# Even layer's seams: statistics later, one more gate block beside the Fourier stage, attention units at a smaller distance, the last heads read last

## The chip, the core and the metric

The kernel runs on one core of one Trainium2 chip. A core has TensorE (PE, the matmuls), VectorE (DVE), ScalarE (ACT), GpSimd (POOL) and SyncE (SP), which issues the DMAs. Each engine works through its own queue in order, and semaphores hold an instruction until what it reads is there. The metric is the device time of one execution, in microseconds (us).

## What is computed

A two-layer encoder over 768 positions (a sequence of 256 and one of 512) and 2048 channels. The change touches layer 0, the even one: one input projection feeds 12 query heads in 4 groups (each with one key and one value head), attention in a window of 128 positions, and 4 groups of Fourier mixing; each branch is multiplied by the SiLU of a gate projection, and one output projection adds to the residual. Cut from the reference:

```python
def _even_layer(x, g, w_in, w_out, q_gain, k_gain, sink, w_f, b_f, rel_bias):
    z = _rmsnorm(x, g) @ w_in
    q, k, v, f, ga, gf = _split(z, EVEN_SPLITS)
    q = _rmsnorm(q.reshape(B, S, N_HEADS, HEAD_DIM), q_gain)
    k = _rmsnorm(k.reshape(B, S, N_KV_HEADS, HEAD_DIM), k_gain)
    a = _window_attention(q, k, v, rel_bias, sink) * jax.nn.silu(ga)
    fo = _fourier(f, w_f, b_f) * jax.nn.silu(gf)
    return x + jnp.concatenate([a, fo], axis=-1) @ w_out
```

## The kernel before

Channels lie on the 128 partitions, positions run along the free axis (T = 768, two halves of H = 384). Every fp32 operand is split into a high and a low part (`split`: a copy on ACT, line 133, and a subtraction on DVE, line 134), and each product is three matmuls (`three`, by `mm`, line 119). The input tiles lie in numbered slots; weights arrive in raw tiles `wr` and are split into `wh` and `wl`, four ahead of their use.

The order on PE is written out by the program: the order of the calls is the order of the queue. Side work is written as generators that a small planner (`Pipe`) holds in a heap. Its clock `pipe.now` counts PE work only: 0.425 ns a column (at least 252 columns) for a matmul, 0.107 a transpose. After each step of the main stream, `tick` runs the generators that are due, and `yield 3.5` means "go on 3.5 units later". `flush` runs what is left, with no main work in between. ACT, DVE and SP are ordered by the scheduler from these calls.

What follows one another in layer 0 around the change:

- The QK pairs and a pair of gates, in a Strassen form (`strassen`). For each of 16 blocks and each half, `Normed.squares` (line 625 on) squares on ACT, adds on DVE, and puts the high and low parts into one tile `st2`; 3.5 units later the matmul with `pick` adds it into one row of `stat`.
- The Fourier stage, pool `fnet`: the roots of the statistics become `rstk` (high part in rows 0 to 15, low part in rows 32 to 47, of 48). `chan_mix` multiplies w_f with the channel transform (L714), `tables` loads and splits the position tables and the Fourier input (`th`, `tl`, `fh`, `fl`), and `fourier` multiplies them. All loads of this stage share four buffers named `row`. Beside it run gate blocks 0 and 1 (`ga_block`, 96 matmuls of 384 columns, of kind `slot,wh` and `slot,wl`, each).
- Attention, pool `attn`: 4 head groups of 6 units. A unit (`attend`) makes its q from `rstk` and a selector `sel` (three matmuls of 48 rows and 128 columns), then scores (`kh,qh`), softmax on DVE and ACT, transposes (`ident,sc`, L129) and products with v (`pth,vh`). Unit i starts at `at - 8 + UNITS_AT * i`. A group's keys take two `rstk,sel` matmuls of 384 columns. After a group's last unit `gates` loads the SiLU gates and multiplies them in (`gate`, L353); for the last group the product is kept on the chip. Gate blocks 2 to 11 are the main stream.
- The first out projection (`Out`): `load_cat` loads and splits the 16 concatenated blocks (two halves each) into slots; the four plain output blocks are done as two duos (`duo`), each by quarters of four blocks; `build_sums` (L394 to L397, and splits) makes the sums for the Strassen pairs after them on DVE.

Of the kernel before, what the change touches and what calls it, by code (L numbers as in the profile page):

```python
# [10 lines left out]
F32 = mybir.dt.float32  # L11
F32R = mybir.dt.float32r
# [5 lines left out]
P = 128  # L18
# [22 lines left out]
QLATE = (2, 3, 0, 1)  # L41
FIRST_UNIT, UNITS_AT = 14.0, 10.2
PT_AT, PV_AT = 7.89, 13.07
# [51 lines left out]
def trunk(ctx, tc, x_t, w_in_e, w_fn, w_vn, w_out_e, w_in_o, w_sv, w_out_o, w_f, w_st, b_s, sink, rel_bias,  # L95
# [62 lines left out]
    nc.scalar.activation(out=pick[:, 15:16], in_=ident[:, 0:1], func=AF.Copy, scale=0.0, bias=1.0)  # L158
    twin = const.tile([48, 16], F32, name="twin")
    nc.vector.tensor_add(out=twin, in0=ident[0:48, 0:16], in1=ident[0:48, 32:48])  # L160
    qg = const.tile([P, 1], F32, name="qg")
# [66 lines left out]
    def out_order(src, layer, pairs):  # L228
        plain = [(src, layer, b, q) for i in range(0, len(PLAIN), 2) for q in range(4) for b in PLAIN[i:i + 2]]
        return plain + [(src, layer, b, q) for b in pairs for q in range(14)]  # L230
# [79 lines left out]
    class Stream:  # L310
# [20 lines left out]

        def duo(self, bs, tags, done):

            for q in range(4):
                weights.ahead(weights.at[self.n, bs[0], q] + RING)
                for k in range(4 * q, 4 * q + 4):
                    for s in range(2):
                        for b, t in zip(bs, (tags[:2], tags[2:])):
                            self.step(b, k, s, t[s], k == 0, k == KT - 1)
                        if done:  # L340
                            done(k, s)
# [30 lines left out]

    def ev():
        return late[-1].tile([P, H], F32, name="ev", bufs=4)

    def extra(dtype=F32):

        return slot(spare[0], dtype) if lent[0] else ev()

# [39 lines left out]
    class Out:  # L419

        def __init__(self, n, pairs, first, last, res, result):
            self.n, self.pairs, self.res, self.result = n, pairs, res, result
            self.tags = (first, last, first)

        def run(self):
# [10 lines left out]
            for i, tags in zip(range(0, len(PLAIN), 2), self.tags):  # L438
                duo = PLAIN[i:i + 2]
                last = i + 2 == len(PLAIN)  # L440
                if last:
                    pipe.flush()
                st.duo(duo, tags, done if last else None)
                for b in duo:
                    for h, z in enumerate(st.take(b)):
                        res = ev()
                        nc.sync.dma_start(out=res, in_=self.res[b][:, SL[h]])
                        nc.vector.tensor_add(out=res, in0=z, in1=res)
                        self.result(b, h, res)
# [140 lines left out]
    with tc.tile_pool(name="early", bufs=1, reuse_waits="tile") as pool:  # L590
# [10 lines left out]
        duo = (GF0, GF0 + 1)  # L601
        st.duo(duo, (6, 7, 0, 1), None)
        for g, b in enumerate(duo):
# [15 lines left out]
        class Normed:  # L619
# [7 lines left out]
            def squares(self, i, h, t):  # L627
# [4 lines left out]
                nc.vector.tensor_add(out=a, in0=a, in1=b)  # L632
                st2 = extra(F32R)
                nc.scalar.copy(out=st2[0:64], in_=a)
                nc.vector.tensor_sub(out=st2[64:P], in0=a, in1=st2[0:64].bitcast(F32))  # L635
                yield 3.5
                mm(stat[h], pick[:, 15 - i:31 - i], st2, i + h == 0 if h == 0 else i == 1, i == 15 - h, True)
# [44 lines left out]
    mid = shared.__enter__()  # L682
    rstk = mid.tile([48, T], F32R, name="rstk")
    banks["z"], banks["s"] = itertools.cycle((0, 1, 4)), itertools.cycle((6, 2, 7, 3, 5))
# [8 lines left out]
    with tc.tile_pool(name="fnet", bufs=1, reuse_waits="tile") as pool:  # L693
        rows.append(pool)
        inv = pool.tile([16, T], F32, name="inv")
        nc.scalar.activation(out=rstk, in_=rr[0:48], func=AF.Copy, scale=0.0)
        for s in range(2):
# [97 lines left out]
        pipe.spawn(tables(), 1.0)  # L795
        pipe.spawn(chan_mix(), 8.0)
        for g in range(NF):
            pipe.spawn(ungated(g), 14.0 + 11.0 * g)
        for j in range(2):
            ga_block(j)  # L800
# [3 lines left out]
    with tc.tile_pool(name="attn", bufs=1, reuse_waits="tile") as pool:  # L804
# [6 lines left out]
        class Group:  # L811
# [5 lines left out]
            def load(self):  # L817
# [6 lines left out]
                for j in range(3):  # L824
# [4 lines left out]
                    self.bias.append(t)  # L829
                self.sel = pool.tile([48, 4, P], F32R, name="sel", bufs=2)  # L830
                e = twin[:, 4 * g:4 * g + 4].rearrange("p (n o) -> p n o", o=1)
                nc.scalar.copy(out=self.sel, in_=e.to_broadcast([48, 4, P]))
                yield 6.0
# [20 lines left out]
        def attend(gr, s, qb):  # L854
# [58 lines left out]
            nc.scalar.copy(out=gr.at[:, :, t * P:(t + 1) * P], in_=ps.rearrange("p (j q) -> p j q", j=3))  # L913
            if (s, qb) == (1, SEQS[1][1] - 1):
                yield 1.0
                gr.gates()

        units = [(s, qb) for s in range(2) for qb in range(SEQS[s][1])]
        for g in range(NKV):
# [3 lines left out]
            for i, (s, qb) in enumerate(units):  # L923
                pipe.spawn(attend(gr, s, qb), at - 8.0 + UNITS_AT * i)
        for j in range(2, NQ):
            ga_block(j)
        pipe.flush()
        load_cat([(k, s) for k in range(KT) for s in range(2)])
    shared.__exit__(None, None, None)
# [12 lines left out]
    sums = {i: [None] * KH for i in (1, 2, 3)}  # L942
    Out(1, PAIRS_E, (2, 3, 6, 7), (0, 1, 4, 5), x_t, keep_sum).run()

# [155 lines left out]
    sums = {i: [None] * KH for i in (1, 2, 3)}  # L1100
    Out(3, PAIRS_O, (0, 1, 4, 5), (2, 3, 6, 7), x1, finish).run()

# [80 lines left out]
```

## Time and profile before

| | |
|---|---|
| median of 3 runs | 2181.46 us (2180.48 to 2181.55) |
| the profiled execution | 2179.42 us, its span 2177.6 us |
| PE busy | 2121.1 us, 97% |
| DVE busy | 1486.3 us, 68% |
| ACT busy | 977.2 us, 45% |
| mean granted clock | 0.988 of full speed |

Times in the profile are us from the span's start. A matmul's end is modelled, so its issue interval is the difference of two starts. The granted clock of TensorE is 1.00 at full speed (2.4 GHz) and 0.50 at half (1.2 GHz); a mean between them says how much of a stretch ran at either. Idle time of an engine counts only if the chain that ends last goes through it.

### The profile page before, as it was taken

To read this page: it belongs to the slowest core of one execution; us is meant where nothing else is said; L and a number is where in the kernel's file an instruction comes from. 1 tells how busy PE (TensorE), PEld (TensorE's weight loads), DVE (VectorE), ACT (ScalarE), POOL (GpSimd) and SP (SyncE) were. 2 spreads that over 40 slices of the span, in tenths; PEclk is the share of its full clock that TensorE was granted. 3 is DMA by queue.
4 is the path that set the end of the run, shared out by engine and by line. 5 is a ranking of instruction groups with operands and counts; after the bars stand their busy time and mean duration, and the time that the engine had idled before them with its cause. 6 is when DMAs were issued, how large, how long until landed. Compare 5 with 4: busy or idle time off the path is not lost.

```text
span 2177.6 us, 32105 instructions
## 1 busy us (share of the span) xinstructions
PE 2121.1 (97%) x11778; PEld 2038.8 (94%) x11778; DVE 1486.3 (68%) x2628; ACT 977.2 (45%) x1907; POOL 75.0 (3%) x75
## 2 busy tenths in 40 slices
PE   8999999989999979999899999999999999999999
PEld 6989999988999979999888999999999999999999
DVE  8686666654566678666695666666666778796665
ACT  6345444543566564333624433333334545553332
POOL 5000000000000000112100000000000000000000
PEclk9999999999999989999999999999999999999999
DMA  6884322354333357433856322222222322394342
GB/s 225 250 296 150 103 90 84 97 165 149 107 127 129 101 199 234 157 117 124 279 187 225 114 85 85 78 77 77 70 85 88 112 92 94 120 318 153 124 136 73
DMA packets 158342, 303.55 MB, mean 139 GB/s; under 512 B 16316, under 2 KB 107624, under 8 KB 158184
## 3 DMA queue, kind: packets, MB, share of 16 engines
q1 hardware_dynamic: 158184, 301.51, 42.9%
q8 instruction: 92, 1.51, 0.3%
q14 instruction: 66, 0.54, 0.1%
HBM read 240.08 MB, written 64.51 MB: 140 GB/s over the span
## 4 chain that ended last, share of the span: by engine, by line
PE 83%; DVE 8%; DMA 3%; ACT 3%; issue 2%; SPq 0%; POOL 0%; ACTq 0%; DVEq 0%
PE bank L119 82%; DVE wl L134 2%; DVE slot L277 1%; PE bank L129 1%; DMA slot<-cat 1%; ACT wh L133 1%; DVE slot L134 1%; DVE slot L635 1%; DVE wr L205 0%; DVE wr L207 0%; ACT sc L888 0%; DMA slot<-x 0%; DMA s<-slot 0%; DMA x<-ev 0%; ACT slot L133 0%
## 5 line engine op out<-in xcount | busy, mean ns | idle before, releaser
L119 PE MATMUL bank<-slot,wh 128*128 128x384 f32 x6448 | 1651.0, 337 | 0.8 <-DVE ev L506 0.8
L119 PEld LDWEIGHTS bank<-slot,wh 128*128 128x128 f32 x6448 | 1164.2, 188 | 4.2 <-issue 2.0
L119 PE MATMUL bank<-slot,wl 128*128 128x384 f32 x3224 | 1084.2, 336 | 3.6 <-DVE wl L134 3.5
L133 ACT CAST wh<-wr 128x512 fp32r<-128x512 f32 x782 | 480.4, 619 | 810.5 <-PE bank L119 628.5
L134 DVE TENSOR_TENSOR wl<-wr,wh 128x512 fp32r<-128x512 f32 x782 | 541.4, 696 | 349.4 <-ACT wh L133 329.8
L119 PEld LDWEIGHTS bank<-slot,wl 128*128 128x128 f32 x3224 | 606.5, 188 | 4.6 <-DVE wl L134 4.6
L119 PE MATMUL bank<-wh,slot 128*128 128x512 f32 x768 | 243.9, 397 | 12.5 <-DVE slot L277 7.3
L119 PEld LDWEIGHTS bank<-wh,slot 128*128 128x128 f32 x768 | 145.9, 190 | 46.0 <-DVE slot L277 9.0
L133 ACT CAST slot<-slot 128x384 fp32r<-128x384 f32 x232 | 114.1, 512 | 141.7 <-DVE slot L134 39.2
L119 PE MATMUL bank<-wl,slot 128*128 128x512 f32 x384 | 152.2, 396 | 1.9 <-DVE wl L134 1.9
L134 DVE TENSOR_TENSOR slot<-slot,slot 128x384 fp32r<-128x384 f32 x232 | 127.8, 556 | 37.8 <-ACT slot L133 32.0
L119 PEld LDWEIGHTS bank<-wl,slot 128*128 128x128 f32 x384 | 73.3, 191 | 18.9 <-DVE wl L134 3.1
L207 DVE TENSOR_TENSOR wr<-wr 128x1024 f32<-128x1024 f32 x45 | 58.4, 1299 | 1.2
L209 DVE TENSOR_TENSOR wr<-wr 128x1024 f32<-128x1024 f32 x45 | 55.1, 1225 | 1.5
L203 DVE TENSOR_TENSOR wr<-wr 128x1024 f32<-128x1024 f32 x45 | 55.0, 1221 | 0.8
L205 DVE TENSOR_TENSOR wr<-wr 128x1024 f32<-128x1024 f32 x45 | 54.9, 1221 | 0.7
L500 DVE TENSOR_TENSOR ev<-bank,ev 128x384 f32<-128x384 f32 x45 | 25.1, 557 | 35.0 <-PE bank L119 34.3
L504 DVE TENSOR_TENSOR ev<-bank,ev 128x384 f32<-128x384 f32 x45 | 25.1, 558 | 31.9 <-PE bank L119 31.9
L509 DVE TENSOR_TENSOR ev<-ev,bank 128x384 f32<-128x384 f32 x45 | 24.9, 553 | 30.0 <-PE bank L119 29.7
L938 POOL TENSOR_TENSOR rr<-rr,slot 128x384 f32<-128x384 f32 x24 | 35.3, 1472 | 132.6 <-ACT slot L937 132.6
L888 ACT ACTIVATE sc<-sc,nm 128x256 f32<-128x256 f32 (+1 forms) x72 | 38.3, 533 | 0.4 <-DVE nm L885 0.3
L877 DVE CUSTOM_DVE_ANT_0 sc<-bank,bias 128x256 f32<-128x256 f32 (+1 forms) x72 | 31.0, 466 | 8.5 <-PE bank L119 8.2
(186 smaller groups left out, 1442.3 us busy)
## 6 DMA issues: line engine op xcount, KB each, us to landing
wr<-in_w_in_o_dram SPq DMA_DIRECT2D x96, 512.0 KB, 3.5
wr<-in_w_in_e_dram SPq DMA_DIRECT2D x64, 512.0 KB, 3.7
slot<-cat SPq DMA_DIRECT2D x120, 192.0 KB, 4.1
wr<-in_w_out_e_dram SPq DMA_DIRECT2D x32, 512.0 KB, 3.8
wr<-in_w_out_o_dram SPq DMA_DIRECT2D x32, 512.0 KB, 3.7
slot<-x SPq DMA_DIRECT2D x64, 192.0 KB, 4.4
wr<-in_w_sv_dram SPq DMA_DIRECT2D x16, 512.0 KB, 4.7
slot<-in_x_t_dram SPq DMA_DIRECT2D x32, 192.0 KB, 4.1
```

The source lines that it names most:

```text
L119: nc.tensor.matmul(out, lhsT=lhs, rhs=rhs, start=start, stop=stop, skip_group_check=go_on)
L133: nc.scalar.copy(out=hi, in_=src)
L134: nc.vector.tensor_sub(out=lo, in0=src, in1=hi.bitcast(F32))
L203: nc.vector.tensor_sub(out=w11, in0=w12, in1=w11)
L205: nc.vector.tensor_sub(out=w11, in0=w22, in1=w11)
L207: nc.vector.tensor_sub(out=w12, in0=w22, in1=w12)
L209: nc.vector.tensor_sub(out=w21, in0=w11, in1=w21)
L500: nc.vector.tensor_add(out=u2, in0=p, in1=r1)
L504: nc.vector.tensor_add(out=r1, in0=p, in1=r1)
L877: nc.vector.tensor_tensor_reduce(out=sc[:, j, :nk * P], in0=ps, in1=gr.bias[j][:, bs], scale=1.0, scalar=NEG, op0=ALU.add, op1=ALU.max, ac ...
L888: nc.scalar.activation(out=sc[:, j, :nk * P], in_=sc[:, j, :nk * P], func=AF.Exp, bias=nm[:, j:j + 1], accum_out=den[:, j:j + 1])
L938: nc.gpsimd.tensor_add(out=rr[:, SL[h]], in0=rr[:, SL[h]], in1=sq)
```

## The change

Five things are changed in layer 0. `squares` waits 6.0 units before its matmul instead of 3.5, and takes every second tile for `st2` from the ring `ev` of four. `rstk`, `sel` and `twin` have 128 rows instead of 48 (the rest zeros). `chan_mix` starts at 12 instead of 8, the Fourier groups at 21 + 10g instead of 14 + 11g, and three gate blocks run beside them instead of two. The first unit starts at 13 instead of 14, and the units are 8.3 apart instead of 10.2, beside nine gate blocks instead of ten. The last head group's gates are multiplied after the flush, and the first duo of the first out projection, its weights and the loads of `cat` take the quarters in the order 0, 1, 3, 2, with the last heads (in quarter 2) last.

```diff
-FIRST_UNIT, UNITS_AT = 14.0, 10.2
+LAST_HEADS = (0, 1, 3, 2)
+FIRST_UNIT, UNITS_AT = 13.0, 8.3
...
-    twin = const.tile([48, 16], F32, name="twin")
-    nc.vector.tensor_add(out=twin, in0=ident[0:48, 0:16], in1=ident[0:48, 32:48])
+    twin = const.tile([P, 16], F32, name="twin")
+    nc.vector.tensor_add(out=twin, in0=ident[:, 0:16], in1=ident[:, 32:48])
...
-        plain = [(src, layer, b, q) for i in range(0, len(PLAIN), 2) for q in range(4) for b in PLAIN[i:i + 2]]
+        qs = LAST_HEADS if layer == 1 else range(4)
+        plain = [(src, layer, b, q) for i in range(0, len(PLAIN), 2) for q in (range(4) if i else qs)
+                 for b in PLAIN[i:i + 2]]
...
-        def duo(self, bs, tags, done):
+        def duo(self, bs, tags, done=None, qs=range(4)):
...
-            for q in range(4):
+            for q in qs:
...
-                            self.step(b, k, s, t[s], k == 0, k == KT - 1)
+                            self.step(b, k, s, t[s], k == 4 * qs[0], k == 4 * qs[-1] + 3)
...
-        return slot(spare[0], dtype) if lent[0] else ev()
+        return slot(spare[0], dtype) if lent[0] else ev(dtype)
...
-                st.duo(duo, tags, done if last else None)
+                st.duo(duo, tags, done if last else None, range(4) if i else self.qs)
...
-                st2 = extra(F32R)
+                st2 = extra(F32R) if i % 2 == h else ev(F32R)
...
-                yield 3.5
+                yield 6.0
...
-    rstk = mid.tile([48, T], F32R, name="rstk")
+    rstk = mid.tile([P, T], F32R, name="rstk")
...
-        nc.scalar.activation(out=rstk, in_=rr[0:48], func=AF.Copy, scale=0.0)
+        nc.scalar.activation(out=rstk, in_=rr, func=AF.Copy, scale=0.0)
...
-        pipe.spawn(chan_mix(), 8.0)
+        pipe.spawn(chan_mix(), 12.0)
         for g in range(NF):
-            pipe.spawn(ungated(g), 14.0 + 11.0 * g)
-        for j in range(2):
+            pipe.spawn(ungated(g), 21.0 + 10.0 * g)
+        for j in range(3):
             ga_block(j)
...
-                self.sel = pool.tile([48, 4, P], F32R, name="sel", bufs=2)
+                self.sel = pool.tile([P, 4, P], F32R, name="sel", bufs=2)
...
-                nc.scalar.copy(out=self.sel, in_=e.to_broadcast([48, 4, P]))
+                nc.scalar.copy(out=self.sel, in_=e.to_broadcast([P, 4, P]))
...
-            if (s, qb) == (1, SEQS[1][1] - 1):
+            if (s, qb) == (1, SEQS[1][1] - 1) and g < NKV - 1:
                 yield 1.0
                 gr.gates()
...
-        for j in range(2, NQ):
+        for j in range(3, NQ):
             ga_block(j)
         pipe.flush()
-        load_cat([(k, s) for k in range(KT) for s in range(2)])
+        gr.gates()
+        load_cat([(k, s) for q in LAST_HEADS for k in range(4 * q, 4 * q + 4) for s in range(2)])
...
-    Out(1, PAIRS_E, (2, 3, 6, 7), (0, 1, 4, 5), x_t, keep_sum).run()
+    Out(1, PAIRS_E, LAST_HEADS, (2, 3, 6, 7), (0, 1, 4, 5), x_t, keep_sum).run()
```

Lines of the changed kernel are numbered 1 higher in the helpers and 3 higher from line 277 on.

On PE in the Fourier stage, from the third of the four chan_mix products (L714) to the first Fourier product (`th,fh`), before:

```order
L714 MATMUL bank<-row 128x128 x2
L119 MATMUL bank<-slot_1849,wh 128x384
L119 MATMUL bank<-slot_1850,wh 128x384
L119 MATMUL bank<-slot_1849,wl 128x384
L119 MATMUL bank<-slot_4522,wh 128x384
L119 MATMUL bank<-slot_4523,wh 128x384
L119 MATMUL bank<-slot_4522,wl 128x384
L119 MATMUL bank<-th_4567,fh_4573 128x258
L119 MATMUL bank<-tl_4568,fh_4573 128x258
```

and now, from the fourth of them (L717):

```order
L717 MATMUL bank<-row 128x128 x2
L120 MATMUL bank<-slot_1637,wh 128x384
L120 MATMUL bank<-slot_1638,wh 128x384
L120 MATMUL bank<-slot_1637,wl 128x384
L120 MATMUL bank<-slot_1687,wh 128x384
L120 MATMUL bank<-slot_1688,wh 128x384
L120 MATMUL bank<-slot_1687,wl 128x384
L120 MATMUL bank<-slot_1815,wh 128x384
L120 MATMUL bank<-slot_1816,wh 128x384
L120 MATMUL bank<-slot_1815,wl 128x384
L120 MATMUL bank<-th_4567,fh_4573 128x258
L120 MATMUL bank<-tl_4568,fh_4573 128x258
```

The Fourier stage's first product moved 43 rows down, behind the end of chan_mix and 39 more rows of gate block; before, the fourth chan_mix product came after the Fourier products.

On PE at the end of attention, from the last scores of one unit to its products with v, before (`ident,sc` x18 are the transposes of two units):

```order
L119 MATMUL bank<-kh,ql 128x384
L119 MATMUL bank<-kh,qh 128x384
L119 MATMUL bank<-kl,qh 128x384
L119 MATMUL bank<-kh,ql 128x384
L129 MATMUL bank<-ident,sc 128x128 x18
L119 MATMUL bank<-pth,vh 128x384
L119 MATMUL bank<-ptl,vh 128x384
L119 MATMUL bank<-pth,vl 128x384
```

and now, around the last unit's transposes (`slot_...` with `wh` or `wl` is gate block 11):

```order
L120 MATMUL bank<-slot_1341,wh 128x384
L120 MATMUL bank<-slot_1342,wh 128x384
L120 MATMUL bank<-slot_1341,wl 128x384
L130 MATMUL bank<-ident,sc 128x128 x6
L120 MATMUL bank<-slot_1393,wh 128x384
L120 MATMUL bank<-slot_1394,wh 128x384
L120 MATMUL bank<-slot_1393,wl 128x384
L120 MATMUL bank<-slot_1533,wh 128x384
L120 MATMUL bank<-slot_1534,wh 128x384
L120 MATMUL bank<-slot_1533,wl 128x384
```

Matmuls of gate block 11 now stand on both sides of the last transposes, where before a unit's scores, the transposes and the products stood one behind the other; 18 of its matmuls also follow the last product with v.

On DVE at the start of the first out projection, from the last gate products (L353, then splits of the kept heads into slots) to the first sums of `build_sums` (L394 on), before:

```order
L894 TENSOR_SCALAR sc<-sc,den 128x256 x3
L904 TENSOR_TENSOR ptl<-bank,pth 128x384 x2
L353 TENSOR_TENSOR at<-row,at 128x768 x3
L134 TENSOR_TENSOR slot_8396<-at,slot_8395 128x384
L134 TENSOR_TENSOR slot_8400<-at,slot_8399 128x384
L134 TENSOR_TENSOR slot_8404<-at,slot_8403 128x384
L134 TENSOR_TENSOR slot_8408<-at,slot_8407 128x384
L134 TENSOR_TENSOR slot_8412<-at,slot_8411 128x384
L134 TENSOR_TENSOR slot_8416<-at,slot_8415 128x384
L134 TENSOR_TENSOR wl<-wr,wh 128x512 x2
L394 TENSOR_TENSOR slot_8490<-slot_8489,slot_8490 128x384
L395 TENSOR_TENSOR slot_8489<-slot_8488,slot_8489 128x384
```

and now (the gate products are L356):

```order
L356 TENSOR_TENSOR at<-row,at 128x768
L135 TENSOR_TENSOR wl<-wr,wh 128x512
L356 TENSOR_TENSOR at<-row,at 128x768
L135 TENSOR_TENSOR slot_8392<-slot_8389,slot_8391 128x384
L135 TENSOR_TENSOR slot_8460<-at,slot_8459 128x384
L135 TENSOR_TENSOR slot_8400<-slot_8397,slot_8399 128x384
L135 TENSOR_TENSOR slot_8464<-at,slot_8463 128x384
L135 TENSOR_TENSOR slot_8468<-at,slot_8467 128x384
L135 TENSOR_TENSOR slot_8472<-at,slot_8471 128x384
L356 TENSOR_TENSOR at<-row,at 128x768
L135 TENSOR_TENSOR wl<-wr,wh 128x512
L135 TENSOR_TENSOR slot_8408<-slot_8405,slot_8407 128x384
```

Before, the three gate products stand together, and 6 splits and two weight tiles follow until the first sum; now they are spread over 10 rows among weights and splits, the first sum (L397) follows 10 rows below the last row shown, and 15 splits lie between the first product and that sum.

## Rows read from the trace of the kernel before

**Rows 1.** The page: busy time and share by engine; the chain that ended last.

```profile
PE 2121.1 (97%) x11778; PEld 2038.8 (94%) x11778; DVE 1486.3 (68%) x2628; ACT 977.2 (45%) x1907; POOL 75.0 (3%) x75
...
PE 83%; DVE 8%; DMA 3%; ACT 3%; issue 2%; SPq 0%; POOL 0%; ACTq 0%; DVEq 0%
```

**Rows 2.** Stretches: length, busy by engine (POOL last), granted clock, DMA share, GB/s.

```profile
185.00:435.00 250.00, 240.85 (x1363) 231.77 (x1362) 167.82 (x248) 123.95 (x225) 0.00 (x0) 1.00 0.31 97
468.00:500.00 32.00, 20.55 (x97) 18.04 (x96) 17.22 (x24) 13.00 (x26) 0.00 (x0) 0.73 0.45 138
570.00:770.00 200.00, 199.61 (x1186) 190.27 (x1185) 126.79 (x375) 122.03 (x275) 0.00 (x0) 1.00 0.38 123
786.00:826.00 40.00, 27.25 (x105) 22.98 (x104) 27.25 (x79) 21.46 (x55) 0.00 (x0) 0.71 0.29 94
835.00:870.00 35.00, 32.86 (x190) 32.54 (x188) 33.13 (x64) 16.34 (x34) 2.37 (x2) 1.00 0.87 279
870.00:880.00 10.00, 9.89 (x48) 9.89 (x49) 5.61 (x11) 4.70 (x11) 0.00 (x0) 0.83 0.84 270
```

**Rows 3.** Waits of PE, 100 to 460: us in total, times, longest.

```profile
PE bank L119 <- DVE slot L635: 8.3, 16, 0.8
```

**Rows 4.** Timeline of PE around a pick matmul: start us, us, operation [idle before].

```profile
202.30 0.51 PE L119 MATMUL bank<-slot,wh 128*128 128x384 f32 x2
202.65 0.34 PE L119 MATMUL bank<-slot,wl 128*128 128x384 f32 x1
203.45 0.35 PE L119 MATMUL bank<-slot,pick 128*16 128x384 f32 x1 [0.47 <-DVE slot L635]
```

**Rows 5.** Timeline of PE: a group of rstk, sel and a unit's transposes.

```profile
567.65 0.34 PE L119 MATMUL bank<-slot,wl 128*128 128x384 f32 x1
567.92 0.55 PE L119 MATMUL bank<-rstk,sel 48*128 48x128 f32 x3
...
568.86 0.35 PE L119 MATMUL bank<-slot,wl 128*128 128x384 f32 x1
...
569.40 0.34 PE L119 MATMUL bank<-slot,wl 128*128 128x384 f32 x1
569.58 0.82 PE L129 MATMUL bank<-ident,sc 128*128 128x128 f32 x6
...
570.59 0.34 PE L119 MATMUL bank<-slot,wl 128*128 128x384 f32 x1
```

**Rows 6.** Timeline of PE in the Fourier stage: what follows each long wait.

```profile
482.14 0.58 PE L119 MATMUL bank<-th,fh 128*128 128x258 f32 x1 [3.76 <-ACT fh L133]
...
486.28 0.58 PE L119 MATMUL bank<-th,fh 128*128 128x258 f32 x1 [2.83 <-ACT fh L133]
...
491.15 0.58 PE L119 MATMUL bank<-th,fh 128*128 128x260 f32 x1 [0.98 <-ACT fh L133]
...
495.24 0.58 PE L119 MATMUL bank<-th,fh 128*128 128x260 f32 x1 [2.77 <-ACT fh L133]
```

**Rows 7.** Groups by shape on PE, 786 to 826: busy, mean ns, idle before.

```profile
L129 PE MATMUL bank<-ident,sc 128*128 128x128 f32 x30 | 6.4, 359 | 5.1 <-DVE sc L894 5.1
```

**Rows 8.** Waits of PE, 775 to 900, columns as in the third group.

```profile
PE bank L119 <- ACT qh L133: 7.1, 3, 4.3
PE bank L129 <- DVE sc L894: 5.1, 2, 4.3
PE bank L119 <- DVE wl L134: 2.3, 1, 2.3
```

**Rows 9.** Timeline of DVE: a unit's three score tiles are scaled.

```profile
566.74 0.88 DVE L894 TENSOR_SCALAR sc<-sc,den 128x256 f32<-128x256 f32 x3
```

**Rows 10.** Timeline of DVE, out projection's start: a wait, first and last.

```profile
833.71 1.29 DVE L134 TENSOR_TENSOR wl<-wr,wh 128x512 fp32r<-128x512 f32 x2 [3.40 <-PE bank L119]
834.92 0.55 DVE L394 TENSOR_TENSOR slot<-slot,slot 128x384 f32<-128x384 f32 x1
...
869.38 0.68 DVE L134 TENSOR_TENSOR wl<-wr,wh 128x512 fp32r<-128x512 f32 x1
```

More of the change, by code (lines that the diff above doesn't have):

```diff
@@ L371, in trunk, with ev @@
     lent = [False]
-    def ev():
-        return late[-1].tile([P, H], F32, name="ev", bufs=4)
+    def ev(dtype=F32):
+        return late[-1].tile([P, H], dtype, name="ev", bufs=4)
     def extra(dtype=F32):
-        return slot(spare[0], dtype) if lent[0] else ev()
+        return slot(spare[0], dtype) if lent[0] else ev(dtype)
     def big(i, dtype=F32):
@@ L419, in trunk, with __init__ @@
     class Out:
-        def __init__(self, n, pairs, first, last, res, result):
-            self.n, self.pairs, self.res, self.result = n, pairs, res, result
+        def __init__(self, n, pairs, qs, first, last, res, result):
+            self.n, self.pairs, self.qs, self.res, self.result = n, pairs, qs, res, result
             self.tags = (first, last, first)
@@ L601, in trunk @@
         duo = (GF0, GF0 + 1)
-        st.duo(duo, (6, 7, 0, 1), None)
+        st.duo(duo, (6, 7, 0, 1))
         for g, b in enumerate(duo):
@@ L1100, in trunk @@
     sums = {i: [None] * KH for i in (1, 2, 3)}
-    Out(3, PAIRS_O, (0, 1, 4, 5), (2, 3, 6, 7), x1, finish).run()
+    Out(3, PAIRS_O, range(4), (0, 1, 4, 5), (2, 3, 6, 7), x1, finish).run()
 def _t5_onehot():
```

## The prediction, made blind

> **What bounds the kernel now.** I read the page first, then a table of stretches, then, in each stretch where TensorE (PE) is not full, the waits of PE and the timeline that shows how long they last. PE is busy 97% of the span and holds 83% of the chain that ended last [rows 1], so time can come only from places where PE stands, runs at a lower clock, or issues more slowly than it could. The table of stretches [rows 2] shows where: in the 200 us of attention from 570 to 770 PE is busy 199.6, but in 468 to 500 (the Fourier stage) only 20.6 of 32 at a granted clock of 0.73, and in 786 to 826 (the last attention units) 27.3 of 40 at 0.71. In 835 to 870 (start of the first out projection) the busy engine is VectorE (DVE): 33.1 of 35.
>
> The profiled execution took 2179.42 us; the median of the runs shown is 2181.46, 2.04 above it. I sum against the profiled one and add the 2.04 at the end.
>
> **Statistics (yield 3.5 to 6.0; st2 in two places).** The list for 100 to 460 has 16 waits of PE on line 635, 8.3 us together [rows 3]. The list counts from modelled ends. By starts it is more: two matmuls of 384 columns start in 0.35, 0.175 each, while the one before the pick matmul takes 0.80, so 0.63 is lost where the list says 0.47 [rows 4]. With that 0.16 on each, 16 waits cost 8.3 + 2.6 = 10.9. The other 16 of the 32 pick matmuls wait too little to be listed; I give them 1 together (0 to 2). The planner counts 0.163 for such a matmul (384 columns at 0.425 ns), so 2.5 more units put the pick 15 matmuls, 2.6 us, later; less the 0.63 that it is late now, 2.0 us are to spare. The second buffer (the ev ring) lets two statistics be in flight; without it the next chain would wait for a later pick. Should that ring be short, some waits come back. **-12** (-13 to -5).
>
> **128 rows instead of 48.** The cost is in the issue gaps. One matmul of the slot kind, three of the rstk kind and two more slots take 1.21 us from 567.65 to 568.86; the same three slots with six 128-row transposes among them take 1.19 from 569.40 to 570.59 [rows 5]. A slot takes 0.18 there (569.40 to 569.58), so 0.67 stays for three rstk matmuls and 0.65 for six transposes, 0.11 each: three of 128 rows would take 0.33, 0.34 less. There are 24 such groups (one a unit) and 8 wider single ones (two a head group), for which I take the same: 32 x 0.34 = 10.9. The work on ACT and DVE that fills the extra rows is done by the same few instructions. Ends: 0, if the rows are not what makes the gap, and -11. The nearest row is the transposes', on the same engine 1.5 us later: **-10**, a little off for the wide ones, which no row prices.
>
> The trace shows gaps on both sides of the 48-row matmuls and none of that size at the 128-row transposes. The Trainium skill ("TensorEngine Tiling (Array Packing)", Key Properties) says that a change of tiling mode drains TensorE, and lists 64-row and 32-row modes. By that rule this term is the whole 10.9; should the rule not be what acts here, it is the rival below with 0.
>
> **Fourier stage (times 12, 21, 10; three gate blocks).** From 468 to 500 PE issued 97 matmuls [rows 2]: 51 of 384 columns (0.175), 30 of 258 or 260 (0.125) and 16 of 128 (0.11, as the transposes [rows 5]) are 14.4 us of work, so 17.6 of the 32 were lost. The waits that open the lost time end at 482.14, 486.28, 491.15 and 495.24, each on a high part of the Fourier input, 4.1 to 4.9 apart [rows 6]. That is the rhythm of the loads, not of PE: tables and input go through four row buffers, of which w_f and chan hold two until chan_mix has ended, before and after alike. The change puts some 43 more matmuls, 7.5 us, ahead of the first Fourier product, so PE starts it near 484.6 instead of 477.1 (six products and the listed 3.76 before 482.14) on the same scale. Then the input that came at 482.14 costs nothing; PE arrives at 485.7 for the one of 486.28 (0.6), at 488.2 for 491.15 (3.0) and at 491.5 for 495.24 (3.7): 7.3 of waits, and with 2.2 for a lower clock behind them 9.5. Gain 17.6 - 9.5 = **-8**. Ends: -14 if the loads move up with the earlier weights, -4 if the third block's loads push them back. The third block's work only changes place.
>
> **Units closer (8.3 for 10.2).** From 786 to 826 PE issued 105 matmuls in 40 us: 30 are transposes of 128 columns [rows 7] at 0.11, 75 take at most 0.175: 16.4, so at least 23.6 us were lost, mostly as waits of 7.1 for qh and 5.1 for sc [rows 8] and at half clock between them. The cause is that the order has no gate-block matmul left between a unit's steps. In the changed order gate block 11 runs until after the last unit's products, with 18 of its matmuls still behind them, so all of this is covered: **-24** (-21 to -25).
>
> The price is a denser stretch. DVE is busy 126.8 and ACT 122.0 of 200 [rows 2]; with units at 8.3/10.2 of their distance that is 63% to at most 78%, and 61% to 75%. A unit's scaled scores end at 567.62, its transposes start at 569.58 [rows 5, 9]: 2.0 us to spare, which more queueing on DVE eats first where a head group changes (splits of v, gates, products). Below nothing there is no end: PE is already full here. Above, 24 units by 0.5 give 12. I take three turns of 1.3, **+4** (0 to +12).
>
> **Last heads read last.** The tail also gave DVE time: the splits that fill cat ran in it. Now they run in a stretch where DVE has less room, and the last gates wait for gate block 11's trip through memory. Between the first of the last gate products and the first sum the DVE order now has 15 splits of 0.55, as the sum there [rows 10], where it had 6: 9 more, 5 us, and the third product waits for gate block 11's gates to be stored and loaded (both ways through one queue, 2 to 5 us more). Of this 3.40 fit into the wait before 833.71. From 834.92 to 869.38 DVE works without a pause worth naming [rows 10], and at its end PE waits 2.3 us for wl [rows 8], with a granted clock of 0.83 over the next 10 us, so 1.7 lost [rows 2]: 4.0 now. A slip of 3.3 to 10 goes straight into that wait. I take 6.5: 2.3 + 6.5 = 8.8, with two falls of the clock (3.4) 12.2, less the 4.0 of now: **+8** (-4 if DVE is early enough, to +12). What hides the reordered quarters is that quarters 0, 1 and 3 (24 of 32 products) stand ahead of the last heads.
>
> **Sum.** -12 - 10 - 8 - 24 + 4 + 8 = -42: 2179.4 - 42 = 2137.4, as a median 2139. All terms at their better ends give -67 (2114), at their worse ones -6 (2175); that all go one way is unlikely.
>
> **Rivals.** *DVE has room* (0.20): the denser units cost 0 and the out projection's wait does not grow beyond what the clock gives back (0): -54 to -58, 2123 to 2127. For it: DVE at 63% in the stretch. Against: 95% in 835 to 870. *DVE becomes the bound* (0.22): +12 in the attention and +12 at the out projection, Fourier -5: -27, 2154 (2147 to 2162). For it: each unit's chain crosses ACT and DVE several times, and both serve weights in between. Against: most of DVE's work there is splits for which PE has a ring of weights. *The rows do not make the gap* (0.09): the 128-row matmuls issue as slowly as the 48-row ones: 2149. For it: rstk differs from the transposes also in its type of data; against: [rows 5]. *The clock falls at every unit* (0.06), which ends slower than before: a wait at each of the 24 transposes long enough that the clock halves. At 1.3 of wait and 1.7 of half clock a unit [rows 2] that is 72 instead of the +4: 2181.5 - 46 + 72, about 2207. From 46/24 = 1.9 us a unit it outweighs the rest. Against it: the waits of about 0.7 in 185 to 435 left the granted clock at 1.00 [rows 2, 3], and 2.0 us are to spare at the transposes. The Trainium skill ("TensorE: Matmul & The Clock Gate", A second HAM failure mode: psum-queue depth-cycling) describes just this, frequent small idle times between groups of matmuls that make the clock swing; in 185 to 435 the trace does not bear it out.
>
> **How the numbers follow.** The forecast has 0.43 with a range of its own of 2129 to 2149. A measurement can tell about 0.2%, 4.4 us, from no change. Forecast, "room", "rows" and all but 0.04 of "bound" are faster by more than that: 0.43 + 0.20 + 0.09 + 0.18 = 0.90. The worst end of "bound" is within 0.2%, 0.04; the clock at every unit is slower, 0.06. The range 2118 to 2162 leaves out that 0.06, the 0.04 and the outer parts of "room" and "bound".
>
> **What would show it.** Statistics: no wait on line 638 (635 now) in 100 to 460. Rows: a group of rstk with its three slots in 0.9 instead of 1.2. Fourier: two waits of 3 to 4 us instead of four. Units: PE full up to the out projection, at a clock of 1.00, with only short waits on sc or qh. Last heads: a wait for wl of 5 us or more some 30 to 45 us into the out projection. It would be wrong if the waits for sc come in every unit, or if the statistics' chain waits for its own buffers.

## The result, and the profile after

The changed kernel takes 2144.48 us (median of 4 runs, 2138.80 to 2146.21) against 2180.97 before (4 runs): a ratio of 0.983, 95% interval 0.981 to 0.985, or 36 us faster. The forecast was 2139, 42 faster, in a range of 2118 to 2162. The profiled execution took 2146.21, its span 2144.4, against 2179.42 and 2177.6.

The page after: PE is at 98%, and the chain that ended last lies 86% on PE, 4% on DVE and 5% on DMAs. Before it was 83%, 8% and 3% [rows 1].

```profile
PE 2095.2 (98%) x11778; PEld 2032.8 (95%) x11778; DVE 1484.2 (69%) x2628; ACT 973.1 (45%) x1904; POOL 75.5 (4%) x75
...
PE 86%; DMA 5%; DVE 4%; ACT 3%; issue 1%; SPq 0%; POOL 0%; DVEq 0%; ACTq 0%
```

The table of stretches shows the stages with their new times. Columns: length, busy time of PE, its weight loads, DVE, ACT and POOL (with instructions), granted clock, DMA share, GB/s.

```profile
185.00:435.00 250.00, 250.00 (x1439) 247.38 (x1438) 173.14 (x255) 126.56 (x230) 0.00 (x0) 1.00 0.31 100
450.00:497.00 47.00, 31.84 (x182) 31.51 (x182) 22.02 (x33) 20.21 (x38) 0.00 (x0) 0.82 0.47 144
570.00:750.00 180.00, 175.99 (x1090) 172.14 (x1089) 129.27 (x402) 117.24 (x286) 0.00 (x0) 1.00 0.40 128
784.00:836.00 52.00, 44.15 (x235) 42.83 (x234) 45.28 (x86) 25.09 (x51) 2.43 (x2) 0.93 0.87 286
```

The QK stage has no idle PE left (250.0 of 250, against 240.9 in [rows 2]). The Fourier stage is as thin as before, 31.8 of 47. In the attention PE waits a little now (176.0 of 180), DVE has gone from 63% to 72%. In the first out projection DVE is busy 45.3 of 52, with PE at 44.2 and a clock of 0.93.

To see where the 33 us of the two profiled executions went, I took the loss of each stage from the starts of PE's matmuls: every interval to the next start, less what one takes undisturbed (set at 0.1733 us for 384 columns, 0.2304 for 512, otherwise 0.45 ns a column and at least 0.06). Both kernels issue the same 11778 matmuls, so these constants drop out of the differences, which are the gain:

```
stage, by PE's order                    before   after   change   forecast
up to the QK stage                        4.8      4.0     -0.8       0
QK stage                                 14.1      1.0    -13.1     -12
last pick to first score (Fourier)       21.8     20.0     -1.8      -8
first score to end of attention          50.2     23.5    -26.7     -30
first out projection                      5.6     13.3     +7.7      +8
everything after                         20.6     21.7     +1.1       0
sum                                     117.1     83.5    -33.6     -42
```

The forecast for the attention is -10 (rows), -24 (tail) and +4 (denser). Four of the five places came out near the forecast. One did not: the Fourier stage.

The list of waits of PE from 460 to 560 has one row, where [rows 6] had four waits:

```profile
PE bank L120 <- ACT row L693: 15.2, 1, 15.2
```

The statistics' waits are gone: the list for 100 to 460 has no row, where [rows 3] had 16 waits. From 560 to 830 (attention and the start of the out projection) the list reads:

```profile
PE bank L120 <- DVE wl L135: 3.7, 2, 2.1
PE bank L120 <- DVE ql L135: 2.6, 4, 1.3
PE bank L120 <- ACT qh L134: 1.0, 1, 1.0
PE bank L120 <- DVE ptl L907: 0.2, 1, 0.2
```

### The profile page after: what moved, and what is told of

The parts are those of the page before. It is cut to its first block, busy times and chain, and to the rows that moved or that the text cites. A ratio compares the mean times of both kernels' runs of the same rounds, so it can differ in the third digit from the quotient of the medians.

```text
span 2144.4 us, 32117 instructions
## 1 busy us (share of the span) xinstructions
PE 2095.2 (98%) x11778; PEld 2032.8 (95%) x11778; DVE 1484.2 (69%) x2628; ACT 973.1 (45%) x1904; POOL 75.5 (4%) x75
## 4 chain that ended last, share of the span: by engine, by line
PE 86%; DMA 5%; DVE 4%; ACT 3%; issue 1%; SPq 0%; POOL 0%; DVEq 0%; ACTq 0%
PE bank L120 86%; DMA slot<-cat 1%; DVE slot L135 1%; DVE slot L280 1%; PE bank L130 1%; DVE wl L135 1%; DMA xr<-in_x_t_dram 1%; DMA s<-slot 0%; ACT slot L279 0%; ACT sc L891 0%; ACT L693 0%; DMA row<-in_seq_s_dram 0%; DMA slot<-x 0%; DMA row<-ga 0%; ACT wh L134 0%
## 5 line engine op out<-in xcount | busy, mean ns | idle before, releaser
L120 PE MATMUL bank<-slot,wh 128*128 128x384 f32 x6448 | 1650.6, 337 | 16.8 <-ACT row L693 15.2
L120 PE MATMUL bank<-wh,slot 128*128 128x512 f32 x768 | 243.3, 396 | 13.1 <-DVE slot L280 7.8
L507 DVE TENSOR_TENSOR ev<-bank,ev 128x384 f32<-128x384 f32 x45 | 25.1, 558 | 31.8 <-PE bank L120 31.8
L906 ACT CAST pth<-bank 128x384 fp32r<-128x384 f32 x56 | 24.1, 483 | 35.2 <-PE bank L130 35.2
```

The lines of the kernel that those rows point to most:

```text
L120: nc.tensor.matmul(out, lhsT=lhs, rhs=rhs, start=start, stop=stop, skip_group_check=go_on)
L507: nc.vector.tensor_add(out=r1, in0=p, in1=r1)
```

## The experiments

Each kernel is the changed one with the edit shown; each was timed in four runs beside its own runs of the kernel before (seven, medians 2178.3 to 2180.7). Times stand against 2144.5, the changed kernel. Its own runs spread over 7 us, so a difference in time under about 4 us is not told from nothing; the losses by stage, from the profiled execution of each, say where a difference lies. They vary too: in the kernels below whose edit does not touch the stage, the Fourier stage loses 17.4 to 20.0 us, the attention 21.7 to 23.5, the out projection 10.9 to 13.9, the QK stage 1.0 or less.

**Statistics undone (u_stats).**

```diff
-                st2 = extra(F32R) if i % 2 == h else ev(F32R)
+                st2 = extra(F32R)
-                yield 6.0
+                yield 3.5
```

> The changed kernel with one part undone: the statistics' matmul 3.5 units after its chain again, and every st2 tile from the one spare slot. If the 13 us that the QK stage lost less are this part's, the waits of PE on line 638 come back (16 listed, some 8.3 us, 13 by starts) and the time is 2144.5 + 13 = 2157.5. Rival: the waits fell because other work around them moved; then they stay away or move, and the time is within 3 us of 2144.5.

2157.33 us, 12.9 slower. The waits of PE from 100 to 460 are those of [rows 3] again, and the QK stage loses 14.2 instead of 1.0:

```profile
PE bank L120 <- DVE slot L638: 8.3, 16, 0.7
```

The delay and the second buffer were undone together, so the share of either is open.

**48 rows again (u_rows).** The edit puts `rstk`, `sel`, `twin` and the two instructions that fill `rstk` and `sel` back to 48 rows.

```diff
-    rstk = mid.tile([P, T], F32R, name="rstk")
+    rstk = mid.tile([48, T], F32R, name="rstk")
...
-                self.sel = pool.tile([P, 4, P], F32R, name="sel", bufs=2)
+                self.sel = pool.tile([48, 4, P], F32R, name="sel", bufs=2)
```

> The changed kernel with rstk, sel and twin at 48 rows again. If the rows make the gap, each of 24 groups of three rstk matmuls with its neighbours takes 1.20 us again instead of 0.85, and 8 wider ones 0.4 more each: 8.4 + 3 = 11.4, so 2156. Rival: the gap belongs to the order around the groups, which is the new one here; then 2144.5 within 3 us and groups at 0.85 to 0.9.

2153.23 us, 8.7 slower. On PE's timeline a group of three in the changed kernel, with 128 rows:

```profile
571.88 0.34 PE L120 MATMUL bank<-slot,wl 128*128 128x384 f32 x1
572.05 0.44 PE L120 MATMUL bank<-rstk,sel 128*128 128x128 f32 x3
572.34 0.39 PE L120 MATMUL bank<-pth,vh 128*128 128x384 f32 x1
572.56 0.33 PE L120 MATMUL bank<-ptl,vh 128*128 128x384 f32 x1
```

and in this one, with 48:

```profile
573.96 0.34 PE L120 MATMUL bank<-slot,wl 128*128 128x384 f32 x1
574.23 0.55 PE L120 MATMUL bank<-rstk,sel 48*128 48x128 f32 x3
574.71 0.44 PE L120 MATMUL bank<-pth,vh 128*128 128x384 f32 x1
574.99 0.34 PE L120 MATMUL bank<-ptl,vh 128*128 128x384 f32 x1
```

The three are followed after 0.29 us (572.05 to 572.34) instead of 0.48 (574.23 to 574.71), and the slot before them after 0.17 instead of 0.27. With the matmul behind them (0.22 instead of 0.28) it is 0.35 a group, as [rows 5] gave 0.34. By starts all 32 groups with their neighbours lose 15.2 us here and 4.2 in the changed kernel: 11.0, close to the 11.4 expected. The time shows less since the waits of the denser stretch shrank in exchange: losses of over 0.15 us away from these groups add up to 3.8 in the attention, against 6.9 in the changed kernel.

**Fourier times undone (u_ftimes).** The three gate blocks stay. With two, the gates of a head group would be read before their gate block is done, so the number of blocks by itself was not tried.

```diff
-        pipe.spawn(chan_mix(), 12.0)
+        pipe.spawn(chan_mix(), 8.0)
...
-            pipe.spawn(ungated(g), 21.0 + 10.0 * g)
+            pipe.spawn(ungated(g), 14.0 + 11.0 * g)
```

> The changed kernel with the Fourier stage's times as before (chan_mix at 8, groups at 14 + 11 g), three gate blocks kept. By the prediction (more work ahead of the first product shortens the waits) 8 us slower, 2152, with four waits on fh again. By the trace of the changed kernel the loads of the tables set the end either way, the 15.2 us wait on line 693 only stands in for the four: the stage loses 20 to 22 us as it does now, 2144.5 within 3.

2143.81 us: no difference. The stage loses 21.4 instead of 20.0, which is not told apart either, and in place of the one long wait stand four shorter ones on fh (list of waits of PE, 440 to 560):

```profile
PE bank L120 <- ACT fh L134: 11.1, 4, 4.3
PE bank L717 <- DMA row<-in_chan_dram: 1.7, 1, 1.7
```

The new times moved the waiting from one place of PE's order to another.

**SiLU of gate block 0 in a tile of its own (x_silu).**

```diff
-        g = row_tile()
+        g = rows[-1].tile([P, T], F32, name="gsilu", bufs=1) if j == 0 else row_tile()
```

> The changed kernel, but the SiLU of gate block 0 writes a tile of its own instead of one of the four row buffers. If the row buffer is what holds the SiLU (it reuses the buffer of the last position table), the 15.2 us wait on line 693 goes; PE runs on with gate block 1 and meets the Fourier products about 10 us before their last input, so some 7 of waits on fh and some 2 at half clock stay: 8 to 10 us faster, about 2135. Rival: the bank is held for another reason (the SiLU stands behind the tables' copies in ACT's queue whatever its tile): the wait stays, 2144.5 within 3.

2131.64 us, 12.8 faster (0.978 of before, 0.975 to 0.980). The 15.2 us wait is gone, and the stage loses 9.8 instead of 20.0. What is left is of the kind that the forecast had expected of the change itself, waits on fh (it had 7.3 of them):

```profile
PE bank L120 <- ACT fh L134: 3.9, 2, 3.2
```

**The stage's buffers divided by use (x_split).**

```diff
-        wf = row_tile()[:, :512]
+        wf = pool.tile([P, 512], F32, name="wf")
-        ch = row_tile()[:, :256]
+        ch = pool.tile([P, 256], F32, name="ch")
...
-                    raw = row_tile()[:, :2 * w]
+                    raw = pool.tile([P, 516], F32, name="traw", bufs=3)[:, :2 * w]
...
-                    fraw = row_tile()[:, :512]
+                    fraw = pool.tile([P, 516], F32, name="traw", bufs=3)[:, :512]
```

(and the `row` ring of this stage has two buffers instead of four.)

> The changed kernel with the Fourier stage's four row buffers divided by use, in 3 KB more: w_f and chan in tiles of their own size, tables and input in a ring of three, SiLU and gates in a ring of two. If the loads' rhythm through two buffers sets the end of the stage, a third buffer brings the last input some 5 us earlier than in x_silu, and the stage loses 4 to 6 us instead of 9.8: about 2127. Rival: the rhythm is that of the DMAs or of SP, not of the buffers; then as x_silu, 2131.6 within 3.

2129.92 us, 14.6 faster (0.978, 0.975 to 0.980). Neither the time nor the stage's loss (6.8 instead of 9.8) is clearly told from x_silu's; the waits on fh are 1.8:

```profile
PE bank L121 <- ACT fh L135: 1.8, 2, 1.1
```

**Units 9.3 apart (x_units93).**

```diff
-FIRST_UNIT, UNITS_AT = 13.0, 8.3
+FIRST_UNIT, UNITS_AT = 13.0, 9.3
```

> The changed kernel with units 9.3 apart instead of 8.3. If the gain at the end of attention is that gate block 11 covers the last units, 23 units of distance more leave some 19 units of time uncovered (13 were uncovered before and cost 24 us): the tail loses 25 to 35 us again and the denser stretch's 5 to 7 us of waits shrink: 2165 to 2175. Rival: the gain came from elsewhere (the 128 rows, the later gates): 2140 to 2150.

2148.50 us, 4.0 slower, at the edge of the noise and much less than the 20 to 30 expected. The stages say why: the attention loses 36.6 instead of 23.5, but the out projection 2.2 instead of 13.3. The waits of PE from 740 to 800 are those of an uncovered tail:

```profile
PE bank L120 <- ACT qh L134: 5.2, 3, 2.5
PE bank L130 <- DVE sc L897: 2.9, 1, 2.9
```

and from 775 to 860 only one wait for wl is left:

```profile
PE bank L120 <- DVE wl L135: 1.6, 1, 1.6
```

Cover for PE and time for DVE trade almost one for one here: 13.1 lost in the attention, 11.1 won behind it. Waits on qh and sc, those of the old tail, are back with less cover, and part of what the cover wins is paid back in the out projection. The 25 to 35 expected was scaled from before by time; of the last units here only the last two or three stood uncovered.

**Quarters in natural order (u_heads).** The last gates stay after the flush, as before the flush they would be read ahead of gate block 11.

```diff
-LAST_HEADS = (0, 1, 3, 2)
+LAST_HEADS = (0, 1, 2, 3)
...
-        load_cat([(k, s) for q in LAST_HEADS for k in range(4 * q, 4 * q + 4) for s in range(2)])
+        load_cat([(k, s) for q in range(4) for k in range(4 * q, 4 * q + 4) for s in range(2)])
```

> The changed kernel with the quarters in their natural order 0, 1, 2, 3 (the last head group's gates stay after the flush). If reading the last heads last hides something, PE waits for their products in quarter 2: the third gate product ran 9.4 us into the out projection and its last split 13.4, quarter 2 is read 16.7 into it. By these rows there is still 3 us of room, so 2144.5 within 3. Rival: reading them earlier pulls their splits ahead of others on DVE or leaves too little room: a wait of 3 us or more, 2148 to 2152.

2140.96 us, 3.5 faster, inside the spread of the changed kernel's own runs. No new wait appears; the list of 775 to 860 has only the waits for wl:

```profile
PE bank L120 <- DVE wl L135: 6.4, 4, 2.5
```

**Sums further apart (x_late).**

```diff
-            pipe.spawn(build_sums(load, sums, BUILD, BUILD_AT))
+            pipe.spawn(build_sums(load, sums, BUILD, BUILD_AT), 14.0 if self.n == 1 else 0.0)
```

The kernel that ran holds back the first step of the sums by 14 units and leaves the steps 5 apart; the text on record speaks of their distance, which was not changed. That text also puts two of the waits into the first duo. By PE's order that duo (192 matmuls, 781.7 to 814.9) has no wait; all of them lie in the first two quarters of the second duo, behind the `flush` that puts what is left of the sums ahead of it. As a test of one other order on DVE the run serves all the same.

> The changed kernel with a step of the first out projection's sums every 14 units instead of every 5, so that fewer of their operations stand ahead of a weight's low part in DVE's order in the first duo. DVE's work is the same. If the waits for wl come from the order of DVE's queue (the low part of a weight behind ten sums that could wait), the two waits of the first duo (4.1 by starts) go and the third (4.0) shrinks: 4 to 8 us faster, 2137 to 2140. Rival: DVE lacks the time itself, or the sums are flushed ahead of the second duo and make a heap there: the waits move behind the first duo, 2144.5 within 4 or slower.

2145.21 us: no difference. The waits in the first quarter of the second duo are gone (it loses 0.0 instead of 6.6), and the rest of the out projection has lost as much more (13.2 instead of 6.7; list of 775 to 900):

```profile
PE bank L120 <- DVE wl L135: 9.6, 2, 7.0
```

Between these two orders of DVE's queue only the place of the wait differs, not its length. This is the recorded rival; an order that spreads the sums beyond the flush was not tried.

**Half of the sums on POOL (x_pool).**

```diff
-            nc.vector.tensor_sub(out=a1, in0=a0, in1=a1)
+            side = nc.gpsimd if aside else nc.vector
+            side.tensor_sub(out=a1, in0=a0, in1=a1)
...
-            nc.vector.tensor_sub(out=b0, in0=b0, in1=a0)
+            side.tensor_sub(out=b0, in0=b0, in1=a0)
```

> The changed kernel, but in the first out projection two of the four sums of each step (16 of 32) run on POOL instead of DVE. If DVE's backlog makes the waits for wl at the start of the out projection (8.9 us by starts), 16 x 0.55 = 8.8 us less of it lets nearly all of them go: 6 to 9 us faster, 2136 to 2138. Rival: the loads of cat or the chain of the sums set the time (a POOL operation of this size takes 1.47 us here): the waits stay or become waits for other tiles, 2144.5 or more.

2143.42 us: no difference; the out projection loses 12.9. The groups of instructions from 796 to 836 show what happened to DVE's splits of slots (count, busy time, mean ns). In the changed kernel:

```profile
L135 DVE TENSOR_TENSOR slot<-slot,slot 128x384 fp32r<-128x384 f32 x25 | 13.7, 553 | 2.3 <-DMA s<-slot 1.5 <-ACT slot L134 0.6
```

and with POOL at work beside them:

```profile
L135 DVE TENSOR_TENSOR slot<-slot,slot 128x384 fp32r<-128x384 f32 x21 | 18.6, 898 | 1.9 <-ACT slot L134 1.4
```

21 splits take 18.6 us where 25 took 13.7. By this run alone it stays open whether DVE's load is the cause.

**Half of the sums left out (x_less).** The same two subtractions are not done at all in the first out projection.

```diff
-            nc.vector.tensor_sub(out=a1, in0=a0, in1=a1)
+            if not less:
+                nc.vector.tensor_sub(out=a1, in0=a0, in1=a1)
...
-            nc.vector.tensor_sub(out=b0, in0=b0, in1=a0)
+            if not less:
+                nc.vector.tensor_sub(out=b0, in0=b0, in1=a0)
```

> The changed kernel with part of its computation left out: of the four sums of each step of the first out projection's build_sums, the two that x_pool put on POOL (16 of 32, 0.55 us each on DVE) are not done at all, so S1, S3 and S4 of that layer carry wrong values. If the amount of DVE work is what makes the waits for wl, 8.8 us less of it takes the 13.3 us that the out projection loses down to 4 to 6: 7 to 9 us faster, 2136 to 2138; x_pool then stayed where it was because POOL slowed DVE. Rival: the waits come from the loads or from the sums' chain: 2144.5 within 3.

2134.75 us, 9.7 faster. The out projection loses 3.4 instead of 13.3, and of the waits for wl 0.4 us is left (list of 775 to 900):

```profile
PE bank L120 <- ACT wh L134: 1.1, 1, 1.1
PE bank L120 <- ACT ev L502: 0.5, 1, 0.5
PE bank L120 <- DVE wl L135: 0.4, 1, 0.4
```

8.8 us less work on DVE are worth 9.7 us, with the loads of `cat` as they were: most of the out projection's loss is DVE's load. (The chain of each sum is two operations shorter as well; the waits that went are PE's for wl, which DVE makes behind the sums.)

**Put together (x_best1, x_best2).** Both have x_split's buffers and the quarters in natural order; x_best1 has units 8.6 apart, x_best2 8.3.

> Buffers of the Fourier stage as in x_split, quarters in natural order, units 8.6 apart. By the stage losses: Fourier 6.8 instead of 20.0, quarters -2 to -3, and at 8.6 some 4 us more at the end of attention against 5 to 7 less of waits for wl (at 9.3 it was 13 more and 11 less): 2144.5 - 13 - 3 - 2 = 2126. Rival: spacing and DVE's backlog only trade one for one: 2128 to 2130.

> x_split with the quarters in natural order and units 8.3 apart. If the natural order is 2 to 3 us faster, as u_heads' trace has it (its out projection lost 10.2 instead of 13.3), 2127. Rival: that was the spread between executions: 2130 within 2.

x_best1 took 2126.88 us (0.975 of before, 0.973 to 0.977), x_best2 2131.14 (0.978, 0.976 to 0.979), x_split 2129.92. The three are not told apart by more than 3 or 4 us, and the natural order's gain did not repeat, so nothing shows it to be more than the spread between executions. x_best1 still loses 11.2 in the out projection, with one wait for wl of 6.2:

```profile
PE bank L121 <- DVE wl L136: 6.9, 2, 6.2
```

All three are faster than the changed kernel by 13 to 18 us, and by 49 to 54 than the kernel before.

## Why the prediction was right, and where not

**Statistics (-12).** Right: 13.1 by the trace, 12.9 by undoing it. The list's 8.3 us would have been too little, since it counts from modelled ends; the starts gave the true price. The eight shortest waits, which the list leaves out, were 0.25 to 0.28 each, 2.1 together, the upper end of what I had given them. The ring `ev` caused no wait.

**128 rows (-10).** Right: 0.35 a group in the trace against 0.34 taken from the transposes' row, 11.0 by the starts of all groups, 8.7 in time by undoing it. The rival "the rows do not make the gap" falls with the two timelines above. The Trainium skill ("TensorEngine Tiling (Array Packing)", Key Properties) says that a change of tiling mode drains TensorE. The two timelines agree with it: the gaps of 0.1 us on both sides of the 48-row matmuls are not there at 128 rows. That 48 rows run in another mode no run shows.

**Fourier stage (-8).** Wrong: 1.8, less than that stage varies from kernel to kernel. The step that failed is the one that put 43 more matmuls ahead of the first Fourier product and let PE run through them. The loads' rhythm was read rightly, and PE had the work, but it could not issue it. The timeline of PE in the changed kernel:

```profile
465.40 0.34 PE L120 MATMUL bank<-slot,wl 128*128 128x384 f32 x1
480.90 1.01 PE L120 MATMUL bank<-slot,wh 128*128 128x384 f32 x2 [15.16 <-ACT row L693]
481.71 0.52 PE L120 MATMUL bank<-slot,wl 128*128 128x384 f32 x1
```

PE stands from 465.4 to 480.9, 12 matmuls into gate block 1, and goes on at half clock (granted clock 0.50 from 481.0 to 484.4). What it waits for is a bank that gate block 0's SiLU (L693) must read first. Gate blocks share three banks and take one for each half of the positions, so the second half of the positions in block 1 needs a bank of block 0. The timeline of ACT says when that SiLU ran:

```profile
472.24 0.62 ACT L134 CAST th<-row 128x516 fp32r<-128x516 f32 x1 [2.59 <-DMA row<-in_seq_s_dram]
...
475.73 0.41 ACT L134 CAST th<-row 128x260 fp32r<-128x260 f32 x1 [1.59 <-DMA row<-in_seq_p_dram]
477.48 0.62 ACT L134 CAST fh<-row 128x512 fp32r<-128x512 f32 x1 [1.35 <-DMA row<-f_d]
478.64 0.41 ACT L134 CAST th<-row 128x260 fp32r<-128x260 f32 x1 [0.54 <-DMA row<-in_seq_p_dram]
479.06 1.28 ACT L693 ACT_TABLE_LOAD   x1
480.36 0.49 ACT L693 ACTIVATE row<-bank 128x384 f32<-128x384 f32 x1
```

It ran right behind the last position table's copy, at 480.36. Its output is a `row` tile, the next in the ring of four after all the tables and inputs, and takes the buffer of that last table. So the gate block's bank was tied to the end of the loads through the very buffers that I had named as the loads' rhythm. Before, the same SiLU (L690) ran behind the last input's copy as well, but the Fourier products stood in PE's order ahead of the matmul that needs the bank, so PE showed the waits on fh [rows 6]. ACT before:

```profile
494.57 0.62 ACT L133 CAST fh<-row 128x512 fp32r<-128x512 f32 x1 [2.89 <-DMA row<-f_d]
...
496.50 0.49 ACT L690 ACTIVATE row<-bank 128x384 f32<-128x384 f32 x1
```

x_silu settles it: with another tile the SiLU of block 0 runs 18 us earlier, the wait goes, and 10.2 us less are lost in the stage. ACT in x_silu:

```profile
462.48 0.49 ACT L693 ACTIVATE gsilu<-bank 128x384 f32<-128x384 f32 x1
```

With that one tile the stage's change would have been 12.0, from 21.8 to 9.8, more than the 8 forecast. u_ftimes adds that without it the new times bring nothing; the start of chan_mix and those of the Fourier groups were undone together.

**Units closer (-24, +4).** Right in both: the tail after 786 lost 26.1 by starts and is gone, at the price of waits in the stretch: losses of over 0.15 us, those beside rstk left out, rose from 2.4 to 6.9. The list of 560 to 830 above has them: q (ql and qh, 3.6) and one ptl, while the transposes, on which I had put the slack, did not wait. What moved back is the first link of a unit's chain, its q. In the longest of these waits (1.3, before 624.32) its low part on DVE stood behind a gate product that had itself waited for a load, at the change of a head group, where the prediction had expected the queueing:

```profile
622.58 0.96 DVE L356 TENSOR_TENSOR row<-row,at 128x768 f32<-128x768 f32 x1 [2.88 <-DMA row<-ga]
...
623.74 0.53 DVE L135 TENSOR_TENSOR ql<-qr,qh 128x384 fp32r<-128x384 f32 x1
```

In the next two (1.0 and 0.9) the high part on ACT or the low part on DVE stood behind the softmax of the unit before, once with a SiLU and a weight between. No run takes these apart.

**Last heads (+8).** Right in size, and in cause as far as DVE goes: 5.6 to 13.3, 7.7. PE's waits for wl in the changed kernel's timeline are

```profile
817.52 0.44 PE L120 MATMUL bank<-slot,wl 128*128 128x384 f32 x1 [2.06 <-DVE wl L135]
...
820.00 0.69 PE L120 MATMUL bank<-slot,wl 128*128 128x384 f32 x1 [1.64 <-DVE wl L135]
...
834.22 0.45 PE L120 MATMUL bank<-slot,wl 128*128 128x384 f32 x1 [3.88 <-DVE wl L135]
```

with 2.1, 1.6 and 3.9 us and the clock at half behind two of them (granted clock 0.50 from 820.0 to 823.4 and from 836 to 838). On DVE the last gate product and the first sum came late, and the weights' low parts later still:

```profile
791.07 0.96 DVE L356 TENSOR_TENSOR at<-row,at 128x768 f32<-128x768 f32 x1 [0.97 <-DMA row<-ga]
...
800.28 0.56 DVE L397 TENSOR_TENSOR slot<-slot,slot 128x384 f32<-128x384 f32 x1 [2.40 <-DMA slot<-cat]
...
816.78 0.69 DVE L135 TENSOR_TENSOR wl<-wr,wh 128x512 fp32r<-128x512 f32 x1
...
819.26 0.69 DVE L135 TENSOR_TENSOR wl<-wr,wh 128x512 fp32r<-128x512 f32 x1
```

The first sum now starts 18.6 us into the out projection (which starts at 781.7), where it was 10.9 (834.92 [rows 10], from 824.0): a slip of 7.7, where I had taken 6.5. Just before it DVE waits 2.40 for a load of `cat`. I had put a wait of 5 us or more 30 to 45 us into the out projection; the waits lie 34 to 53 into it, the longest 3.9. The cause was only argued there. x_less shows it: take 8.8 us from DVE, and 9.9 of the loss goes. x_late shows the same loss in another order of the queue, x_units93 that with a longer tail it is nearly gone (2.2). That the order of the quarters hides something was not shown; u_heads and x_best2 found no difference. The last gates' place behind the flush was not undone by itself.

**Rivals.** "DVE has room" fell on the out projection. "DVE becomes the bound" was half right in place, with 7.7 instead of 12 in the out projection and 4.5 instead of 12 in the attention, by the waits of over 0.15 us. "The clock falls at every unit" did not happen: 1.00 from 570 to 750, with waits on q of up to 1.3 us.

The table's 33.6 fall 8.4 short of the 42: 6.2 by the Fourier stage and 3.3 by the attention; the other places, about 1 off each at most, add up to 1.1 the other way. The medians differ by 36. The time lies in the range although one of the five mechanisms failed, since the range of 44 us is far wider than that term; the time alone would not have shown it.

## What to carry to other kernels

When work is moved ahead of a wait to fill it, check what that work itself must get back (a bank, a buffer) and from whom: if its own release hangs on the thing waited for, the wait only moves. A ring of buffers that serves two streams ties the faster one to the slower one; a tile more for one use was worth 12.8 us here, where the new times alone brought nothing. And time that an engine off the critical path had in a tail has to be found again when the tail is closed: of the 26 us that closing it won, 8 were paid back in the next stage, where the one other order of the queue that was tried saved nothing and less work did.

## What was not expected of the hardware

An operation of POOL can hold up one of DVE. In x_pool a split of slots on DVE that takes 0.55 us alone takes 1.39 when a POOL subtraction starts 0.03 ahead of it. On DVE:

```profile
802.58 0.55 DVE L397 TENSOR_TENSOR slot<-slot,slot 128x384 f32<-128x384 f32 x1
803.29 1.39 DVE L135 TENSOR_TENSOR slot<-slot,slot 128x384 fp32r<-128x384 f32 x1 [0.17 <-ACT slot L134]
804.61 0.55 DVE L400 TENSOR_TENSOR slot<-slot,slot 128x384 f32<-128x384 f32 x1
```

and on POOL:

```profile
803.26 1.01 POOL L399 TENSOR_TENSOR slot<-slot,slot 128x384 f32<-128x384 f32 x1 [1.62 <-ACT slot L134]
```

The split ends at 804.68, 0.41 after POOL's end at 804.27, as if it had stood still for most of POOL's 1.01 us. Over 21 splits the mean rose from 553 to 898 ns, and 16 operations taken off DVE bought nothing. The Trainium skill ("SBUF — State Buffer", SBUF: two separate sides) says that DVE and GpSimd share a pair of ports as an exclusive lock, which an operation of DVE with two SBUF inputs needs as well, against a GpSimd operation that reads SBUF. These rows agree with it.
